# GpSimd keeps its part of the modulation sum in an accumulator of its own

## The chip, the core and the metric

The kernel runs on one core of a Trainium2 chip. The core's engines each run their own instructions in a fixed order: TensorE (PE, with its weight loads as PEld), VectorE (DVE), ScalarE (ACT), GpSimd (POOL) and SyncE (SP), which issues most of the transfers. The metric is the device time of one execution in microseconds (us); lower is better.

## The reference, cut to what matters

Two layers of a backbone over 512 latent tokens and 256 context tokens of width 1024. Ahead of each layer a modulation vector is computed from the conditioning, once for the latents and once for the context; it scales and shifts the normalised input and gates the layer's output. In the second layer only the latents go on to the output, so the gate part of its modulation is needed for them alone.

```
mod = silu(c) @ mod_w + mod_b          # 1024 -> 3 x 1024: shift, scale, gate; also for c_ctx
h   = rmsnorm(x) * (1 + scale) + shift
z   = h @ w_in                          # one projection: attention, pool, GLA, gates, merge
y_m = softmax_attention(...) * silu(z_mla_gate)     # 8 heads
y_p = multiscale_pool(...)   * silu(z_pool_gate)
y_g = gla_scan(...)          * silu(z_gla_gate)     # both directions
merged = sum over branches b of sigmoid(z_merge_b) * (y_b @ w_branch_b)
x   = x + gate * rmsnorm(merged @ w_out)
```

## The kernel before

Everything is kept in fp32 precision: an operand is split into a high and a low half (wh, wl), and a product is three matmuls. Each layer runs through stages: input projection, gated linear attention (GLA) with the pooling mixer, the softmax attention, the merge of the three branches, the output projection. Within a stage the parts of several kinds of work are interleaved: beside the attention of layer l, PE computes the blocks of the merge gates (zA_m), whose weights come as 512 KB blocks raw_m through SP, are split by ACT (wh_m) and DVE (wl_m), and leave PE by way of ACT (st_m) and a transfer (sm).

The modulation of a layer has twelve chunks of 256 columns, j = 0 to 11; j = 8 to 11 are the gate. Layer 0's first eight are done by PE at the start. The other sixteen are done "beside PE" (`chunk_beside_pe`, L210): layer 0's j = 8 to 11 and layer 1's j = 0 to 7 for two streams (latents and context), layer 1's j = 8 to 11 for one. A chunk is eight tiles of 128 rows of mod_w, brought as two loads of 512 KB (raw_mod). Each tile is multiplied by a column of silu(c) and added into the accumulator macc. DVE does multiply and add in one instruction; POOL takes the odd tiles of the last stream and does a multiply in place (raw_mod, L230) and an add (macc). Both add into the same accumulator, so each waits for the other at every step. At the end PE sums the accumulator over its 128 partitions by a matmul with a column of ones (modt), two per stream. `columns` (L167) adds the bias; for the gate chunks it also writes the result to a buffer in DRAM, grow, by one transfer for each stream on POOL's queue (L179), element by element. The output stage reads it back as pg (L264).

The steps of these chunks are drawn by hand from a generator, `next(todo_mod)`. Drawing a step starts a chunk (its loads and its sums) and finishes the one before it (modt, columns, grow). In layer 0 there is a step after all but a few of the 24 gate blocks (the condition at L911) and one after the last, sixteen in all; in layer 1 a step after each of the four pairs of blocks of the p branch (L998) and one after the branches (L1001). From the emitted program a scheduler makes the engines' orders, with priorities (`urgent`) and a pool's buffers as limits: a tile of a pool with n buffers must wait until the n-th last one of its name is free.

Three pools matter here. `stream` has three buffers under the name raw, through which go raw_m, raw_mod, the branches' weights (raw_wbp, raw_wbg, raw_wbm) and the branches' inputs as they are read back (yrp, yrg, yrm). `small` lasts for the whole program and holds macc. `att{l}` is opened with the attention of layer l (L740) and holds, among much else, ys (two buffers), a half of a head's output on its way from PSUM to ypair.

Of the kernel before, what the change touches and what calls it, by code (L numbers as in the profile page):

```python
# [11 lines left out]
F32 = mybir.dt.float32  # L12
# [6 lines left out]
P = 128  # L19
D = 1024  # L20
KD = 8
# [27 lines left out]
def hybrid_kernel(ctx, tc, io, out):  # L49
# [23 lines left out]
    def stt(out, a, s, b, op0=ALU.mult, op1=ALU.mult):  # L73
        return V.scalar_tensor_tensor(out=out, in0=a, scalar=s, in1=b, op0=op0, op1=op1)  # L74
# [29 lines left out]
    def load_raw(src, nk, width, name, pool=stream):  # L104
        raw = pool.tile([P, nk, width], F32, tag="raw", name=f"raw_{name}", bufs=3 if pool is stream else None)
        nc.sync.dma_start(out=raw, in_=src)
        return raw
# [46 lines left out]
    def modulation(l, pool=None):  # L154


        cols = const.tile([P, 24, 2], F32, tag=f"mcols{l}", name=f"mcols{l}")
        grow = dram.tile([2, D], F32, name=f"grow{l}")
        mods[l] = (cols, grow)
        modb = small.tile([P, 24], F32, tag="modb", name=f"modb{l}", bufs=1)  # L160
        nc.gpsimd.dma_start(out=modb, in_=io["mod_b"][l])
        pre = small.tile([P, KD], F32, tag="pre", name=f"pre{l}", bufs=1)
        nc.gpsimd.dma_start(out=pre, in_=io["pre_norm"][l])
        post = small.tile([P, KD], F32, tag="post", name=f"post{l}", bufs=1)
        nc.gpsimd.dma_start(out=post, in_=io["post_norm"][l])

        def columns(j, pt, streams=2):  # L167

            at = slice(2 * j, 2 * j + 2)
            dst = cols[:, at, 0:streams]  # L170

            def spread(v, c0):
                return v[:, 2 * j - c0:2 * j - c0 + 2].unsqueeze(2).to_broadcast([P, 2, streams])

            tt(dst, pt[:, :, 0:streams], spread(modb, 0), ALU.add)
            if j >= 8:
                tt(dst, dst, spread(post, 16))
                for st in range(streams):
                    nc.gpsimd.dma_start(out=grow[st].rearrange("(b p) -> p b", p=P)[:, 2 * j - 16:2 * j - 14], in_=dst[:, :, st])  # L179
            elif j >= 4:  # L180

                stt(dst, dst, 1.0, spread(pre, 8), ALU.add, ALU.mult)

        def chunk_on_pe(j):
            parts = j in (5, 6, 3, 7)
            ps = pst.tile([4 if parts else 2, 256], F32, tag="t", name=f"modps{l}_{j}")
            for half in range(2):
                raw = pool.tile([P, 4, 256], F32, tag="raw", name=f"raw_mod{l}_{j}_{half}", bufs=10)
                nc.sync.dma_start(out=raw, in_=io["mod_w"][l, j][:, 4 * half:4 * half + 4, :])
                if parts:  # L190
                    wh = pool.tile([P, 4, 256], F32R, tag="xin", name=f"mwh{l}_{j}_{half}", bufs=6)
                    wl = pool.tile([P, 4, 256], F32R, tag="xin", name=f"mwl{l}_{j}_{half}", bufs=6)
                    act(wh, raw)
                    tt(wl, raw, wh.bitcast(F32), ALU.subtract)
                for k in range(4):
                    kk = 4 * half + k
                    if parts:
                        mm(ps, chl[:, kk, :], wh[:, k, :], kk == 0, False)
                        mm(ps[0:2], chl[:, kk, 0:2], wl[:, k, :], False, kk == KD - 1)
                    else:  # L200
                        mm(ps, csil[:, kk, :], raw[:, k, :], kk == 0, kk == KD - 1)
            n = 4 if parts else 2
            row = pool.tile([n, 256], F32, tag="modrow", name=f"modrow{l}_{j}")
            act(row, ps)
            pt = psz.tile([P, 2, 2], F32, tag="z", name=f"modt{l}_{j}")
            for i in range(2):
                mm(pt[:, i], row[:, i * P:(i + 1) * P], sel[0:n], True, True)
            columns(j, pt)

        def chunk_beside_pe(j):  # L210

            streams = 2 if j < 8 or l < DEPTH - 1 else 1
            acc = small.tile([P, 2, 256], F32, tag="macc", name=f"macc{l}_{j}", bufs=1)
            for half in range(2):
                raw = load_raw(io["mod_w"][l, j][:, 4 * half:4 * half + 4, :], 4, 256, f"mod{l}_{j}_{half}")
                for k in range(4):
                    kk = 4 * half + k
                    for st in range(streams):
                        c = csil[:, kk, st:st + 1]
                        w, a = raw[:, k], acc[:, st]  # L220
                        eng = (G if streams == 1 and kk%2 else V) if st==0 else (G if kk%2 else V)
                        if kk == 0:
                            (eng if eng is G else V).tensor_scalar(out=a, in0=w, scalar1=c, scalar2=None, op0=ALU.mult)
                        elif eng is V:
                            stt(a, w, c, a, ALU.mult, ALU.add)
                        else:
                            if eng is S:
                                act(w, w, scale=c)
                            else:
                                G.tensor_scalar(out=w, in0=w, scalar1=c, scalar2=None, op0=ALU.mult)  # L230
                            tt(a, a, w, ALU.add, G)
            yield
            pt = psz.tile([P, 2, 2], F32, tag="z", name=f"modt{l}_{j}")
            for i in range(2):
                for st in range(streams):
                    mm(pt[:, i, st:st + 1], acc[:, st, i * P:(i + 1) * P], ones, True, True)
            columns(j, pt, streams)


        pend = []  # L240
        for j in (0, 4, 1, 5, 2, 6, 3, 7, 8, 9, 10, 11):
            if pool is not None and j < 8:
                chunk_on_pe(j)
            else:
                pend.append(chunk_beside_pe(j))
                next(pend[-1])
                if len(pend) > 1:
                    next(pend.pop(0), None)
            if j == 11 or (pool is None and j == 7):
                yield  # L250
                for chunk in pend:
                    next(chunk, None)
                pend = []
            yield

    mods = {}

    def gate_rows(l, pool, streams):

# [89 lines left out]
    def layer(l, hT, close_hT, side, todo_mod):  # L349
# [387 lines left out]


        g2 = ExitStack()
        ap = g2.enter_context(opened(f"att{l}", 2, side))  # L740
        pss = g2.enter_context(opened(f"pss{l}", 1, None, MemoryType.PSUM))
        psu = g2.enter_context(opened(f"psu{l}", 2, None, MemoryType.PSUM))
        qn = ap.tile([P, 2], F32, tag="qn", name=f"qn{l}", bufs=1)
# [114 lines left out]
        def weighted_sum(head, q0, nk):  # L858
            pth, ptl = pt_h.pop((head, q0))
            j = head % 2  # L860
            vv = vvs[head // 4]
            av = pst.tile([P, 256], F32, tag="t", name=f"av{l}_{head}_{q0}")
            for kt in range(nk):
                st_ = vv[:, kt, head % 4].rearrange("p s d -> p (s d)")
                mm(av, st_, pth[:, kt, :], kt == 0, False)
                mm(av, st_, ptl[:, kt, :], False, kt == nk - 1)
            if (head, q0) == (head, groups[0][0]) and j == 0:
                yps[head // 2] = ap.tile([P, T], F32, tag="ypair", name=f"ypair{l}_{head // 2}", bufs=1)
            ypair = yps[head // 2]
            rows = slice(64 * j, 64 * j + 64)  # L870
            oth = slice(64 - 64 * j, 128 - 64 * j)
            ys = ap.tile([P, 256], F32, tag="ys", name=f"ys{l}_{head}_{q0}")
            act(ys[rows], av[oth])
            tt(ypair[rows, q0 * P:q0 * P + 256], av[rows], ys[rows], ALU.add)
            if j == 1 and q0 == groups[-1][0]:
                pair = head // 2
                sg = ap.tile([P, T], F32, tag="qf", name=f"sgm{l}_{pair}", bufs=1)
                nc.gpsimd.dma_start(out=sg[:, lo:T], in_=sg_d["m"][pair][:, lo:T])
                tt(ypair[:, lo:T], ypair[:, lo:T], sg[:, lo:T])
                if full or pair < 3:  # L880
                    nc.gpsimd.dma_start(out=y_d["m"][pair][:, lo:T], in_=ypair[:, lo:T])
# [26 lines left out]
        for nm in ("m1", "m2", "m0"):  # L908
            for i in range(8):
                gate_block(nm, i, sm_d[nm], tanh_out if nm in early_gates else stage_out)  # L910
                if full and n_mod >= 6 and n_mod % 6 != 3:  # L911
                    next(todo_mod, None)
                n_mod += 1

# [331 lines left out]
```

## Time and profile before

| | |
|---|---|
| runs shown | 1511.17, 1519.75 and 1519.8 us; median 1519.75 us |
| the profiled execution | 1523.7 us, of it 1521.9 us from the first to the last instruction |
| mean granted TensorE clock | 0.982 of full speed |

The stages and how busy PE is in them, by the windows of the trace:

| us | stage | PE busy | PE clock |
|---|---|---|---|
| 0 to 60 | start, modulation on PE | 50.12 | 1.00 |
| 60 to 425 | layer 0: projection, GLA, pooling mixer | 360.92 | 0.99 to 1.00 |
| 425 to 720 | layer 0: attention, gate blocks, p branch begins | 273.20 of 295 | 0.97 |
| 720 to 870 | layer 0: branches, output | 146.61 of 150 | 1.00 |
| 870 to 1340 | layer 1: up to its attention | 458.95 of 470 | 0.99 |
| 1340 to 1410 | layer 1: p and g branches beside the attention's end | 59.17 of 70 | 0.90 |
| 1410 to 1522 | layer 1: branches, output | 100.08 of 112 | 0.98 |

In the prediction, a row of a group reads: line, engine, operation, tile written <- tiles read, shape, count | busy us, mean ns of one | idle us of the engine just before them, and the releaser that ended most of it. In a timeline row the first number is the start, the second the length, and the square bracket is the idle time before it. A transfer's number is the time from issue to landing.

### The profile page before, as it was taken

Reading aid. Unit: us, or ns where it says so; the run is one execution under the profiler, and the core shown is the slowest. Engines: PE = TensorE matmul, PEld = TensorE weight load, DVE = VectorE, ACT = ScalarE, POOL = GpSimd, SP = SyncE. Lnnn points to the kernel's source line nnn. Section 1 sums busy time; section 2 is a strip of 40 time slices with the busy share of each in tenths; the row PEclk is TensorE's granted clock in tenths of the full one; section 3 lists DMA queues with packets and bytes.
Section 4 is the critical chain, followed back from the end, with each engine's and each line's share of the span. In section 5 each row is a group of like instructions: output and inputs, shape, how many; then the busy total and the mean of one; then the engine's idle time right before and its main releaser. Section 6 shows DMA issues by size and latency. Waiting matters only on the chain. (4 is left out here: it accounts for less than half of the span.)

```text
span 1521.9 us, 23904 instructions
## 1 busy us (share of the span) xinstructions
PE 1449.1 (95%) x8940; PEld 1282.7 (84%) x8940; DVE 1069.9 (70%) x1980; ACT 718.5 (47%) x1340; POOL 525.4 (35%) x695
## 2 busy tenths in 40 slices
PE   7999999999997999998999989999999999997988
PEld 3799899998886889887879978988988888886878
DVE  3645999757575788876675374689976676686783
ACT  6554453443343445656443346554253555454532
POOL 3431433454243344552111074424553000063450
PEclk9999999999998999999999999999999999998999
DMA  9333333255544632446555233434256423158631
GB/s 366 105 118 118 101 101 115 89 165 191 180 77 99 140 121 89 137 139 183 172 196 201 79 116 117 155 117 126 90 177 215 153 95 95 51 156 152 222 127 68
DMA packets 64195, 209.75 MB, mean 138 GB/s; under 512 B 12464, under 2 KB 15696, under 8 KB 64080
## 3 DMA queue, kind: packets, MB, share of 16 engines
q1 hardware_dynamic: 38688, 116.74, 25.3%
q0 software_dynamic: 24528, 88.34, 18.0%
q10 hardware_dynamic: 864, 3.15, 0.5%
q8 instruction: 70, 1.15, 0.3%
q14 instruction: 45, 0.37, 0.1%
HBM read 161.65 MB, written 46.54 MB: 137 GB/s over the span
## 5 line engine op out<-in xcount | busy, mean ns | idle before, releaser
L89 PE MATMUL zA_m<-hh,wh_m 128*128 128x512 f32 (+1 forms) x576 | 206.3, 358 | 1.1 <-ACT wh_m L68 1.1
L89 PE MATMUL zA_m<-hh,wl_m 128*128 128x512 f32 (+1 forms) x576 | 205.9, 358 | 0.6 <-DVE wl_m L71 0.6
L89 PE MATMUL zA_m<-hl,wh_m 128*128 128x512 f32 (+1 forms) x576 | 206.3, 358 | 0.0
L89 PEld LDWEIGHTS zA_m<-hh,wh_m 128*128 128x128 f32 x576 | 109.7, 190 | 16.0 <-ACT wh_m L68 1.5
L89 PEld LDWEIGHTS zA_m<-hh,wl_m 128*128 128x128 f32 x576 | 109.5, 190 | 15.4 <-DVE wl_m L71 1.1
L89 PEld LDWEIGHTS zA_m<-hl,wh_m 128*128 128x128 f32 x576 | 109.6, 190 | 14.3
L68 ACT ACTIVATE wh_m<-raw_m 128x1024 fp32r<-128x1024 f32 x48 | 50.9, 1060 | 93.4 <-PE zA_m L89 40.7
L68 ACT ACTIVATE pe<-sc,mx 128x768 f32<-128x768 f32 (+1 forms) x80 | 65.2, 815 | 61.3 <-DVE mx L830 60.7
L71 DVE TENSOR_TENSOR wl_m<-raw_m,wh_m 128x1024 fp32r<-128x1024 f32 x48 | 58.9, 1226 | 47.1 <-ACT wh_m L68 46.6
L230 POOL TENSOR_SCALAR raw_mod<-raw_mod,csil 128x256 f32<-128x256 f32 x64 | 70.5, 1106 | 61.5 <-DVE macc L74 39.4
L830 DVE TENSOR_REDUCE mx<-sc 128x1 f32<-128x768 f32 (+1 forms) x80 | 67.6, 845 | 34.1 <-PE sc L89 33.5
L74 DVE SCALAR_TENSOR_TENSOR macc<-raw_mod,csil,macc 128x256 f32<-128x256 f32 x132 | 71.6, 552 | 10.9 <-POOL macc L71 9.2
L68 ACT ACTIVATE pth<-pt 128x256 fp32r<-128x256 f32 (+1 forms) x144 | 62.0, 472 | 31.9 <-PE pt L852 31.4
L71 DVE TENSOR_TENSOR ptl<-pt,pth 128x256 fp32r<-128x256 f32 (+1 forms) x144 | 72.5, 533 | 6.0 <-ACT pth L68 4.8
L89 PEld LDWEIGHTS lv<-pqk 128*128 128x128 f32 x560 | 70.9, 191 | 4.6 <-issue 1.8
L89 PE MATMUL lv<-pqk 128*128 128x128 f32 x560 | 73.4, 275 | 1.2 <-DVE pqk L71 1.1
L346 POOL DMA_DIRECT2D sm<-st_m x32 | 17.6, 550 | 161.9 <-ACT st_m L68 144.5
L89 PE MATMUL sc<-kth,qth 96*128 96x256 f32 (+1 forms) x144 | 50.4, 350 | 24.0 <-ACT pe L68 24.0
L71 POOL TENSOR_TENSOR macc<-macc,raw_mod 128x256 f32<-128x256 f32 x64 | 55.5, 868 | 35.5 <-DVE macc L74 29.8
L89 PE MATMUL br_p<-yp,wh_wbp 128*128 128x512 f32 (+1 forms) x192 | 56.6, 379 | 6.7 <-ACT yp L68 5.8
L852 PE MATMUL pt<-ident,pe 128*128 128x128 f32 x416 | 61.3, 273 | 0.3 <-DVE pe L839 0.2
L89 PE MATMUL zB_gv<-wh_gv,hh 128*128 128x256 f32 x192 | 55.3, 290 | 5.1 <-ACT st_gv L68 2.9
(402 smaller groups left out, 4746.2 us busy)
## 6 DMA issues: line engine op xcount, KB each, us to landing
raw_mod<-in_mod_w SPq DMA_DIRECT2D x48, 512.0 KB, 5.2
raw_m<-in_w_in SPq DMA_DIRECT2D x48, 512.0 KB, 3.7
sm<-st_m POOLq DMA_DIRECT2D x24, 384.0 KB, 3.0
raw_wo<-in_w_out SPq DMA_DIRECT2D x16, 512.0 KB, 3.9
sm<-st_m POOLq DMA_DIRECT2D x24, 256.0 KB, 2.5
raw_gv<-in_w_gv SPq DMA_DIRECT2D x8, 512.0 KB, 3.8
raw_gg<-in_w_in SPq DMA_DIRECT2D x8, 512.0 KB, 4.0
raw_px<-in_w_in SPq DMA_DIRECT2D x8, 512.0 KB, 4.0
```

The costliest lines, as they stand in the source:

```text
L68: return S.activation(out=out, in_=in_, func=func, **kw)
L71: return (eng or V).tensor_tensor(out=out, in0=a, in1=b, op=op)
L74: return V.scalar_tensor_tensor(out=out, in0=a, scalar=s, in1=b, op0=op0, op1=op1)
L89: PE.matmul(out=out, lhsT=lhsT, rhs=rhs, start=start, stop=stop)
L230: G.tensor_scalar(out=w, in0=w, scalar1=c, scalar2=None, op0=ALU.mult)
L346: nc.gpsimd.dma_start(out=dst[:, lo:T], in_=st[:, lo:T])
L830: V.tensor_reduce(out=mx, in_=ps[:, 0:nkey], axis=AX.X, op=ALU.max, negate=True)
L852: PE.transpose(out=pt[:, kk, :], in_=pe[:, (k0 + kk) * P:(k0 + kk + 1) * P], identity=ident)
```

## The change

The accumulator gets a third row, acc[:, 2]. Where the last stream's tile is odd, POOL multiplies the first one (kk = 1) into that row and adds the later ones to it; DVE's part stays in acc[:, st]. PE puts the two together with a second matmul into the same result. macc moves from the pool `small` to the attention's pool, reached through `beside[0]`; with three rows it is 3 KB a partition, and ys there gets one buffer for two. The condition on the steps in layer 0 is another: it leaves out the first four blocks and every third, so that fourteen steps are drawn there, not sixteen. The chunks j = 8 and 9 of layer 1 thereby begin in layer 1's p branch, and j = 11 is finished by the last step, after the branches.

```diff
-            acc = small.tile([P, 2, 256], F32, tag="macc", name=f"macc{l}_{j}", bufs=1)
...
+            acc = beside[0].tile([P, 3, 256], F32, tag="macc", name=f"macc{l}_{j}", bufs=1)
+            for kk in range(KD):
+                if kk % 4 == 0:
+                    raw = load_raw(io["mod_w"][l, j][:, kk:kk + 4, :], 4, 256, f"mod{l}_{j}_{kk // 4}")
+                w = raw[:, kk % 4]
+                for st in range(streams):
+                    c = csil[:, kk, st:st + 1]
+                    if st == streams - 1 and kk % 2:
+                        a = acc[:, 2]
+                        G.tensor_scalar(out=a if kk == 1 else w, in0=w, scalar1=c, scalar2=None, op0=ALU.mult)
+                        if kk > 1:
                             tt(a, a, w, ALU.add, G)
+                    elif kk == 0:
+                        V.tensor_scalar(out=acc[:, st], in0=w, scalar1=c, scalar2=None, op0=ALU.mult)
+                    else:
+                        stt(acc[:, st], w, c, acc[:, st], ALU.mult, ALU.add)
             yield
             pt = psz.tile([P, 2, 2], F32, tag="z", name=f"modt{l}_{j}")
             for i in range(2):
+                at = slice(i * P, (i + 1) * P)
                 for st in range(streams):
-                    mm(pt[:, i, st:st + 1], acc[:, st, i * P:(i + 1) * P], ones, True, True)
+                    both = st == streams - 1
+                    mm(pt[:, i, st:st + 1], acc[:, st, at], ones, True, not both)
+                    if both:
+                        mm(pt[:, i, st:st + 1], acc[:, 2, at], ones, False, True)
             columns(j, pt, streams)
...
+    beside = [None]
...
-        ap = g2.enter_context(opened(f"att{l}", 2, side))
+        ap = beside[0] = g2.enter_context(opened(f"att{l}", 2, side))
...
-            ys = ap.tile([P, 256], F32, tag="ys", name=f"ys{l}_{head}_{q0}")
+            ys = ap.tile([P, 256], F32, tag="ys", name=f"ys{l}_{head}_{q0}", bufs=1)
...
-                if full and n_mod >= 6 and n_mod % 6 != 3:
+                if full and n_mod >= 4 and n_mod % 3 != 2:
                     next(todo_mod, None)
```

What this does to the engines' orders is seen at three places. The first is ACT in layer 0's attention, just after the second gate chunk (j = 9) has been finished and its two grow transfers issued. Before:

```order
L68 ACTIVATE ys_0_2_4103<-av_0_2_4089 64x256
L68 ACTIVATE wh_m_0_6521<-raw_m_0_6519 128x1024
L68 ACTIVATE pe_0_4_1_3970,sm_0_4_1_3971<-sc_0_4_1_3961,mx_0_4_1_3968 128x768
L68 ACTIVATE qth_1_4047<-qf_1_4026 96x768
L68 ACTIVATE st_m_0_6515<-zA_m_0_256_6465 128x512
```

And with the change:

```order
L68 ACTIVATE pe_0_4_0_3955,sm_0_4_0_3956<-sc_0_4_0_3946,mx_0_4_0_3953 128x768
L68 ACTIVATE wh_m_0_6462<-raw_m_0_6460 128x1024
L68 ACTIVATE st_m_0_6456<-zA_m_0_256_6406 128x512
L68 ACTIVATE pe_0_4_1_3970,sm_0_4_1_3971<-sc_0_4_1_3961,mx_0_4_1_3968 128x768
L68 ACTIVATE qf_1_4026<-qps_1_256_4027 64x512
```

In both, the split of a freshly loaded weight block (wh_m) stands ahead of the exponentials (pe) of the same piece of the attention; the chunk now ends somewhat earlier in the attention.

The second is SP at the end of layer 0, where the last mod loads, the first weights of the p branch (raw_wbp) and its inputs (yrp) follow one another. Before:

```order
L106 DMA raw_m_0_7602<-in_w_in 128x1024
L106 DMA raw_mod_8_0_7663<-in_mod_w 128x1024
L106 DMA raw_mod_8_1_7671<-in_mod_w 128x1024
L106 DMA raw_mod_9_0_7680<-in_mod_w 128x1024
L106 DMA raw_mod_9_1_7688<-in_mod_w 128x1024
L106 DMA raw_wbp_0_7714<-in_w_branch_p 128x1024
L934 DMA yrp_0_7720<-yp_552 128x768
```

With the change:

```order
L106 DMA raw_mod_7_0_7574<-in_mod_w 128x1024
L106 DMA raw_mod_7_1_7585<-in_mod_w 128x1024
L106 DMA raw_m_0_7605<-in_w_in 128x1024
L106 DMA raw_wbp_0_7686<-in_w_branch_p 128x1024
L938 DMA yrp_0_7692<-yp_552 128x768
```

The four loads of layer 1's chunks 8 and 9 have left this place.

The third is SP in layer 1's p branch, from its last yrp on. Before:

```order
L934 DMA yrp_3_14619<-yp_9671 128x512
L106 DMA raw_mod_10_0_14657<-in_mod_w 128x1024
L106 DMA raw_mod_10_1_14665<-in_mod_w 128x1024
L106 DMA raw_wbp_1_14679<-in_w_branch_p 128x1024
L106 DMA raw_wq_7_13468<-in_w_uq 128x256
L106 DMA raw_mod_11_0_14718<-in_mod_w 128x1024
L106 DMA raw_mod_11_1_14726<-in_mod_w 128x1024
L106 DMA raw_wbp_2_14740<-in_w_branch_p 128x1024
L106 DMA raw_wbp_3_14784<-in_w_branch_p 128x1024
L106 DMA raw_wbg_0_14822<-in_w_branch_g 128x1024
```

With the change:

```order
L106 DMA raw_mod_8_1_14636<-in_mod_w 128x1024
L106 DMA raw_wbp_1_14644<-in_w_branch_p 128x1024
L106 DMA raw_wq_7_13440<-in_w_uq 128x256
L106 DMA raw_mod_9_0_14683<-in_mod_w 128x1024
L106 DMA raw_mod_9_1_14690<-in_mod_w 128x1024
L106 DMA raw_wbp_2_14706<-in_w_branch_p 128x1024
L106 DMA raw_mod_10_0_14745<-in_mod_w 128x1024
L106 DMA raw_mod_10_1_14752<-in_mod_w 128x1024
L106 DMA raw_wbp_3_14768<-in_w_branch_p 128x1024
L106 DMA raw_mod_11_0_14807<-in_mod_w 128x1024
L106 DMA raw_mod_11_1_14814<-in_mod_w 128x1024
L106 DMA raw_wbg_0_14830<-in_w_branch_g 128x1024
```

Two mod loads now stand between any two weight blocks of the p branch. On POOL the grow of layer 1's last chunk, which stood within the branches, now stands behind the four ml subtractions ahead of the output projection, and pg directly behind it.

More of the change, by code (lines that the diff above doesn't have):

```diff
@@ L212, in chunk_beside_pe @@
             streams = 2 if j < 8 or l < DEPTH - 1 else 1
-            acc = small.tile([P, 2, 256], F32, tag="macc", name=f"macc{l}_{j}", bufs=1)
[L214 to L230, printed above, removed]
+            acc = beside[0].tile([P, 3, 256], F32, tag="macc", name=f"macc{l}_{j}", bufs=1)
[9 more added lines that the diff above has]
+                        if kk > 1:
                             tt(a, a, w, ALU.add, G)
+                    elif kk == 0:
+                        V.tensor_scalar(out=acc[:, st], in0=w, scalar1=c, scalar2=None, op0=ALU.mult)
+                    else:
+                        stt(acc[:, st], w, c, acc[:, st], ALU.mult, ALU.add)
             yield
```

## The prediction

> **What bounds the kernel now.** I read the page from the top: engine shares first, then the groups with the idle time ahead of them.
>
> ```profile
> span 1521.9 us, 23904 instructions
> PE 1449.1 (95%) x8940; PEld 1282.7 (84%) x8940; DVE 1069.9 (70%) x1980; ACT 718.5 (47%) x1340; POOL 525.4 (35%) x695
> L230 POOL TENSOR_SCALAR raw_mod<-raw_mod,csil 128x256 f32<-128x256 f32 x64 | 70.5, 1106 | 61.5 <-DVE macc L74 39.4
> L74 DVE SCALAR_TENSOR_TENSOR macc<-raw_mod,csil,macc 128x256 f32<-128x256 f32 x132 | 71.6, 552 | 10.9 <-POOL macc L71 9.2
> L89 PE MATMUL sc<-kth,qth 96*128 96x256 f32 (+1 forms) x144 | 50.4, 350 | 24.0 <-ACT pe L68 24.0
> L71 POOL TENSOR_TENSOR macc<-macc,raw_mod 128x256 f32<-128x256 f32 x64 | 55.5, 868 | 35.5 <-DVE macc L74 29.8
> L89 PE MATMUL br_p<-yp,wh_wbp 128*128 128x512 f32 (+1 forms) x192 | 56.6, 379 | 6.7 <-ACT yp L68 5.8
> ```
>
> PE is busy 95% of the span, so only what adds PE work or opens and closes its 73 us of gaps can move the time. GpSimd's waits in the shared accumulator look large (39.4 + 29.8 us), but PE does not wait for them: the groups with idle time on PE are sc (24.0 us, behind ScalarE's pe) and br_p (5.8 us, behind ScalarE's yp). So I asked where these two sit, through the waits, the timeline and the transfers of the windows around them.
>
> ```profile
> PE sc L89 <- ACT pe L68: 10.8, 1, 10.8
> 463.90 1.06 ACT L68 ACTIVATE wh_m<-raw_m 128x1024 fp32r<-128x1024 f32 x1 [14.43 <-DMA raw_m<-in_w_in]
> 464.98 0.90 ACT L68 ACTIVATE pe<-sc,mx 128x768 f32<-128x768 f32 x1
> DMA to landing us min/median/max: 3.1/3.7/16.6
> L179 POOL DMA_DIRECT2D grow<-mcols x12: 716/741/776, 428.8 to 1392.3; - x12
> DMA to landing us min/median/max: 4.0/9.2/16.6
> ```
>
> The first row is PE's wait at 466 us, the longest of sc. ScalarE runs in order: it stood 14.43 us at wh_m for a weight load, with the pe that PE needed queued behind. That load, issued at 447 us, is the longest of its kind: 16.6 us, where raw_m takes 3.7 us at the median (fourth row, the tile view of raw_m). The last two rows are the tile view of grow: twelve writes of one KB or less, one element of four bytes at a time, with a median landing of 9.2 us (the three pg loads are counted in it) and one of 16.6. A pair of them was in the air at 446 us. The other gaps have the same neighbour:
>
> ```profile
> yrp<-yp SPq DMA_DIRECT2D x4, 384.0 KB, 6.4
> grow<-mcols POOLq DMA_DIRECT2D x1, 1.0 KB, 9.0
> 699.95 0.50 PE L89 MATMUL sc<-kth,qth 96*128 96x512 f32 x1 [1.15 <-ACT pe L68]
> 707.91 1.52 PE L89 MATMUL br_p<-yp,wh_wbp 128*128 128x512 f32 x3 [5.60 <-ACT yp L68]
> 1369.58 11.55 DMA raw_wbp<-in_w_branch_p
> 1383.14 0.80 PE L89 MATMUL sc<-kth,qth 96*128 96x512 f32 x1 [5.38 <-ACT pe L68]
> 1392.05 9.82 DMA raw_wbg<-in_w_branch_g
> 1403.88 0.50 PE L89 MATMUL sc<-kth,qth 96*128 96x512 f32 x1 [2.53 <-ACT pe L68]
> 466.03:470.30 4.27, 4.27 (x18) 4.08 (x19) 3.79 (x9) 1.82 (x5) 2.03 (x2) 0.50 0.37 123
> 705.90:712.70 6.80, 4.79 (x14) 4.07 (x15) 5.58 (x12) 5.37 (x12) 0.72 (x1) 0.50 0.84 277
> 1381.70:1391.90 10.20, 8.36 (x23) 6.82 (x24) 9.38 (x14) 7.86 (x15) 5.40 (x5) 0.50 0.56 151
> 1405.60:1409.00 3.40, 3.40 (x9) 2.67 (x8) 3.40 (x6) 2.00 (x3) 2.24 (x4) 0.50 0.89 257
> ```
>
> Rows 1 and 2 are transfers issued between 690 and 712 us, at the end of layer 0. Rows 5 and 7 are pieces of the chain of waits in layer 1's branches. The last four are the windows table (us, PE busy, PEld, DVE, ACT, POOL, granted clock, DMA share, GB/s): after each long gap the granted clock is 0.50, and half of PE's busy time there is loss. The price of a place is its gap plus this half: at 446 us 10.8 + 2.1 = 12.9 us; at 696 us 1.15 + 5.60 + 2.4 = 9.2 us; in layer 1 5.38 + 2.53 + 4.2 + 1.7 = 13.8 us, for three grows, 4.6 each. So my reading is: grow writes hold up the loads issued behind them, and a load that ScalarE meets in its order stops PE. The change is worth what it does to these places.
>
> **The change part by part.**
>
> *Sixteen POOL adds fewer.* The first odd tile's product now is the accumulator: 64 adds become 48, 16 x 0.868 = 13.9 us of POOL, which is 35% busy. The mutual waits go (9.2 us on DVE; POOL's are not on PE's path). PE gains at most what sc waits outside the places above: 24.0 - 10.8 - 1.15 - 5.38 - 2.53 = 4.1 us, and DVE's other work stays. Bounds 0 and -4.1; I take -2, the middle, since no row ties these waits to macc.
>
> *The sum of the two accumulators on PE.* Two more matmuls a chunk, 32 in all, each seen as two rows:
>
> ```profile
> L89 PE MATMUL modt<-ones,macc 128*128 128x1 f32 x112 | 14.1, 237 | 0.0
> ```
>
> Before there are 56 matmuls in 112 rows, so 64 rows come. By busy time a row costs 14.1/112 = 0.126 us: +8.1 us. Bounds: 0 if they fell into gaps, 64 x 0.237 = 15.2 if none overlapped. PE is 95% busy and they stand in its order: +8.1.
>
> *macc in the attention's pool.* The chunk j=8 of layer 0, which before began in the pooling mixer, cannot begin until that pool opens.
>
> ```profile
> L223 DVE TENSOR_SCALAR macc<-raw_mod,csil x28: 325/346/428, 368.8 to 1364.5; 128x256 f32<-128x256 f32 x28
> 368.00:425.00 57.00, 57.00 (x334) 50.31 (x334) 35.38 (x66) 22.62 (x37) 19.97 (x27) 1.00 0.51 172
> 368.00:640.00 272.00, 257.18 (x1591) 228.88 (x1591) 206.61 (x423) 124.44 (x262) 112.56 (x131) 0.97 0.46 123
> ```
>
> PE had no gap from 368 to 425 us, so nothing is gained there. DVE's part of this chunk, 14 x 0.552 + 2 x 0.346 = 8.4 us, moves into a stretch where DVE is already busy 206.61 of 272. Between 0 and +8.4: +1, nearer to nothing, since a tenth or so of DVE's delay has reached PE (the 9.2 us above against PE's small waits).
>
> *ys in one buffer.* The next ys waits for the add that reads the last one.
>
> ```profile
> L71 DVE TENSOR_TENSOR ypair<-av,ys x40: 397/422/429, 454.0 to 1453.4; 64x256 f32<-64x256 f32 x40
> ```
>
> Behind a waiting ys on ScalarE stand pe and pth. The wait is at most one add, 0.42 us: 0 to 40 x 0.42 = 17 us. I take 0, because the 40 come over a thousand us, some 25 us apart at the mean.
>
> *The pairs of layer 0's attention (j = 8 to 11).* Four pairs remain. In the order, the weight loads stand behind the second pair as before, so I keep one hit and shorten it: 16.6 was the longest landing; at 9.2 ScalarE is released 7.4 us sooner, which leaves 10.8 - 7.4 + 2.1 = 5.5 us, and 2 more for small hits of the other three. 7.5 against 12.9: -5. Bounds: -12.9 (none hit) and +12.9 (another one hit in full).
>
> *The end of layer 0.* Two chunks (layer 1's j = 8 and 9) leave it: four 512 KB loads ahead of raw_wbp and yrp in SP's queue, and the one grow behind which yrp landed late. ScalarE's yp and then br_p come sooner. 0 to -9.2; -9.2, because yrp has nothing else to wait for.
>
> *Layer 1's branches.* SP now brings eight mod loads between the p branch's four weight loads, not four, through the same ring of three; three grows (j = 8, 9, 10) stay, the last one goes to the end.
>
> ```profile
> 1361.21 1.24 POOL macc L71
> 1362.46 3.97 DMA raw_wbp<-in_w_branch_p
> raw_mod<-in_mod_w SPq DMA_DIRECT2D x48, 512.0 KB, 5.2
> 1340.00:1410.00 70.00, 59.17 (x307) 49.64 (x306) 52.21 (x95) 34.06 (x66) 32.71 (x38) 0.90 0.70 162
> ```
>
> The first two rows, from the chain: a weight load issued only when POOL's last macc gave a ring slot back. Four more loads can cost 0 to 4 x 5.2 = 20.8 us; PE is idle 10.8 of these 70 us, so much of that is exposed already. I take one load, +5. The grows at their old price: 0.
>
> *The last grow.* It stands on POOL's queue behind the last ml, with pg behind it.
>
> ```profile
> 1472.37 1.60 POOL L71 TENSOR_TENSOR ml<-acc,mh 128x512 fp32r<-128x512 f32 x1 [1.89 <-ACT mh L68]
> DMA to landing us min/median/max: 4.0/4.5/4.7
> L71 DVE TENSOR_TENSOR part<-part,pg x4: 684/691/695, 1484.9 to 1494.0; 128x512 f32<-128x512 f32 x4
> 1491.45 1.23 DVE L71 TENSOR_TENSOR wl_wo<-raw_wo,wh_wo 128x1024 fp32r<-128x1024 f32 x1 [0.67 <-ACT wh_wo L68]
> ```
>
> 1474.0 + 9.2 + 4.5 (pg, second row) = 1487.7, 2.8 us after the first part add. Three adds of 0.69 then end at 1489.8, ahead of wl_wo at 1491.45, on which PE depends: 0. At 16.6 it is 1495.1 and costs up to 5.7.
>
> Sum: -2 + 8.1 + 1 + 0 - 5 - 9.2 + 5 + 0 = -2.1 us on the profiled execution, whose run took 1523.7 us. The median of the runs shown is 1519.75, so 1517.6 us.
>
> **The rivals.**
>
> *B, slower: layer 1's ring jams.* If the four loads are exposed whole, layer 1 costs 20.8 instead of 5, 15.8 more: 1533.4. If the last grow before the g branch also holds yrg as the one at 1369 held raw_wbp (5.38 + 4.2 = 9.6), 1543.0. Middle 1538. For it: the slot wait in the chain, and PE idle there already. Against: each chunk gives its slot back sooner. It decides once PE waits over 15 us more in these branches.
>
> *C, faster: no grow meets a load that matters.* The pairs cost 0 (-12.9, not -5) and layer 1's half (-6.9, not +5): 1517.6 - 7.9 - 11.9 = 1497.8. For it: before there were grows at eight places (four pairs, four single ones), and PE's long gaps stand at four. Against: the loads still follow the grows closely.
>
> *D: layer 0's end gains nothing,* because yrp is held by another wait: 1526.8. Against it stands the 9.0 us grow beside a yrp of 6.4.
>
> *E: the two accumulators block each other.* Uncoupled, POOL's multiplies and DVE's accumulation run at the same time more often. In the trace DVE's instruction spans 552 ns at the mean:
>
> ```profile
> L74 DVE SCALAR_TENSOR_TENSOR macc<-raw_mod,csil,macc x132: 457/479/1550, 370.4 to 1383.5; 128x256 f32<-128x256 f32 x132
> ```
>
> so all slowing now is at most 132 x (552 - 457) = 12.5 us. If each one met half of a POOL add (0.43 us), it would be 57 us, 45 more on DVE; at the tenth that has reached PE, +4.5 instead of -2: 1524.1. The Trainium skill's page "SBUF — State Buffer", section "Who interferes with whom", speaks against the change in this way: a VectorE instruction with two SBUF inputs contends with a GpSimd instruction that reads SBUF, and the loser of the port stands still for the whole instruction. By that rule the sum would be E's; the median of 479 ns beside the 1550 ns longest shows that it happens, but not to half of the instructions.
>
> **How the numbers follow.** The likeliest, 0.43, is 1517.6, with 1508 to 1528 its own range. B 0.21, C 0.24, D 0.06, E 0.06. The range 1495 to 1541 takes in C's value and B's middle, and leaves out about a third of each, 0.15. A measurement of this kernel tells about 1% (15.2 us) from no change: faster is below 1504.6, slower above 1535. Faster: 0.20 of C and 0.05 of the likeliest's tail, 0.25. Slower: 0.16 of B and 0.03 of D, E and the rest, 0.19. Same: 0.56.
>
> **What would show it.** modt has 176 rows of about 22 us in all; POOL's macc adds number 48 and nothing waits DVE to POOL on macc; br_p waits no 5.6 us at layer 0's end and yrp lands in some 3 us; a load behind a grow still takes 9 us or more. Layer 1's 70 us become 75, with raw_wbp issued when a mod slot is freed. The forecast is wrong if PE's long waits stand somewhere else, above all if a pair of grows meets other loads than before, or if pg is late at the end.

## The result, and the profile after

| | before | after |
|---|---|---|
| median of the runs | 1519.78 us (4 runs) | 1542.56 us (1540.85 to 1549.89, 4 runs) |
| span of the profiled execution | 1521.9 us | 1541.9 us |
| granted clock | 0.982 | 0.979 |

The ratio is 1.0167 with a 95% interval of 1.0135 to 1.0199: slower by some 22.8 us. The forecast was 1517.6 us; the result lies just above the range.

The head of the page after, and of its groups those that answer to the ones shown of before:

```profile
span 1541.9 us, 24019 instructions
PE 1461.4 (95%) x9004; PEld 1291.9 (84%) x9004; DVE 1070.3 (69%) x1980; ACT 718.4 (47%) x1340; POOL 504.2 (33%) x679
L223 POOL TENSOR_SCALAR raw_mod<-raw_mod,csil 128x256 f32<-128x256 f32 x48 | 54.0, 1127 | 70.7 <-DVE macc L74 56.5
L74 DVE SCALAR_TENSOR_TENSOR macc<-raw_mod,csil,macc 128x256 f32<-128x256 f32 x132 | 68.2, 540 | 0.9
L89 PE MATMUL br_p<-yp,wh_wbp 128*128 128x512 f32 (+1 forms) x192 | 54.6, 370 | 6.1 <-ACT wh_wbp L68 4.6
L89 PE MATMUL modt<-ones,macc 128*128 128x1 f32 x176 | 21.6, 236 | 0.5 <-POOL macc L71 0.4
```

The change does what it says: DVE's idle time ahead of its accumulation falls from 10.9 to 0.9 us, and POOL is 21 us less busy. POOL's multiply still waits for DVE, because it overwrites a tile that DVE, for the other stream, must have read. PE's own waits (the waits view; us in total, times, longest) have moved:

```profile
PE sc L89 <- ACT pe L68: 7.8, 6, 4.3
PE pt L856 <- ACT pe L68: 7.6, 1, 7.6
PE zB_wo L89 <- DVE mcols L71: 7.2, 1, 7.2
PE zA_m L89 <- ACT wh_m L68: 4.9, 2, 4.4
PE br_p L89 <- ACT wh_wbp L68: 4.6, 1, 4.6
```

The one wait of 10.8 us is gone, and so is br_p's wait of 5.8 us for yp; five others of 4 to 8 us have come.

To see where the time came from I cut each execution at work that every version does: at the first sc of layer 0, the first transpose for layer 1, the last zA_m of layer 1 and the last br_m. "Stalls" is PE's idle time, plus half of PE's busy time where the granted clock is 0.5; "work" is the rest.

| piece (us) | before: length = stalls + work | after |
|---|---|---|
| start to layer 0's attention | 426.5 = 17.1 + 409.5 | 425.9 = 16.6 + 409.3 |
| layer 0: attention, branches, output | 447.3 = 31.5 + 415.9 | 449.8 = 27.8 + 422.0 |
| layer 1 up to its last gate block | 460.0 = 15.4 + 444.6 | 459.1 = 13.2 + 445.9 |
| layer 1: p branch to the last br_m | 128.7 = 17.3 + 111.5 | 141.4 = 26.9 + 114.5 |
| to the end | 59.3 = 11.3 + 48.0 | 65.7 = 18.4 + 47.3 |

Of 20 us in the spans, 12.7 lie in layer 1's branches and 6.4 behind them. Layer 0, where the prediction had most of the gain, is 2.5 us longer: 6.1 us more work, and only 3.7 us fewer stalls. The pieces are of one profiled execution each. The changed kernel and the kernel of the second experiment below (PSUM) have the same orders up to layer 1's branches, and yet their first two pieces differ by 2.0 and 3.3 us; a difference of that size between two kernels says little.

### The profile page after: what moved, and what is told of

It reads as the page before. It is cut to its first block, busy times and chain, and to the rows that moved or that the text cites. A ratio compares the mean times of both kernels' runs of the same rounds, so it can differ in the third digit from the quotient of the medians.

```text
span 1541.9 us, 24019 instructions
## 1 busy us (share of the span) xinstructions
PE 1461.4 (95%) x9004; PEld 1291.9 (84%) x9004; DVE 1070.3 (69%) x1980; ACT 718.4 (47%) x1340; POOL 504.2 (33%) x679
## 4 chain that ended last, share of the span: by engine, by line
PE 63%; DVE 16%; DMA 9%; issue 5%; POOL 3%; ACT 3%; SPq 0%; DVEq 0%; POOLq 0%; ACTq 0%
PE zA_m L89 15%; PE zB_gv L89 4%; PE zB_wo L89 4%; PE zA_mg L89 4%; DMA raw_m<-in_w_in 4%; PE wo L89 3%; PE sc L89 3%; PE zA_pg L89 2%; PE zA_gk L89 2%; PE br_m L89 2%; PE lv L89 2%; PE zA_px L89 2%; PE br_p L89 2%; DVE pqk L71 2%; PE zB_qkv L89 2%
## 5 line engine op out<-in xcount | busy, mean ns | idle before, releaser
L89 PEld LDWEIGHTS zA_m<-hl,wh_m 128*128 128x128 f32 x576 | 109.3, 190 | 14.4
L223 POOL TENSOR_SCALAR raw_mod<-raw_mod,csil 128x256 f32<-128x256 f32 x48 | 54.0, 1127 | 70.7 <-DVE macc L74 56.5
L74 DVE SCALAR_TENSOR_TENSOR macc<-raw_mod,csil,macc 128x256 f32<-128x256 f32 x132 | 68.2, 540 | 0.9
L856 PEld LDWEIGHTS pt<-ident,pe 128*128 128x128 f32 x416 | 50.9, 145 | 14.2 <-ACT pe L68 7.8
L89 PE MATMUL br_g<-yg,wh_wbg 128*128 128x512 f32 (+1 forms) x192 | 55.1, 367 | 4.4 <-ACT yg L68 3.2
```

The costliest lines, as they stand in the source:

```text
L89: PE.matmul(out=out, lhsT=lhsT, rhs=rhs, start=start, stop=stop)
L223: G.tensor_scalar(out=a if kk == 1 else w, in0=w, scalar1=c, scalar2=None, op0=ALU.mult)
L856: PE.transpose(out=pt[:, kk, :], in_=pe[:, (k0 + kk) * P:(k0 + kk + 1) * P], identity=ident)
```

## The experiments

**First question: is it the steps or the accumulator?** The theory was that the moved steps (theory S) make the loss. One kernel has the accumulator with the steps of before, one the steps with the accumulator of before.

```diff
 (own accumulator, old steps)
-            acc = beside[0].tile([P, 3, 256], F32, tag="macc", name=f"macc{l}_{j}", bufs=1)
+            acc = small.tile([P, 2, 256], F32, tag="macc", name=f"macc{l}_{j}", bufs=1)
+            if streams == 2:
+                own = beside[0].tile([P, 256], F32, tag="macg", name=f"macg{l}_{j}", bufs=1)
+            else:
+                own = acc[:, 1]
...
-                if full and n_mod >= 4 and n_mod % 3 != 2:
+                if full and n_mod >= 6 and n_mod % 6 != 3:
 (the kernel before, new steps)
-                if full and n_mod >= 6 and n_mod % 6 != 3:
+                if full and n_mod >= 4 and n_mod % 3 != 2:
```

> GpSimd's own accumulator, the second matmul and the single ys buffer stay; the steps are drawn as before (16 in layer 0). Because layer 1's chunks 8 and 9 then begin in layer 0, macc stands in the small pool as before and only the two-stream chunks' third row in the attention's pool. Theory S (the moved steps cost the 22.8 us, in layer 1's branches +12.6 and behind them +6.4): 1516 to 1529 us, layer 1's stretch from the p branch to the last br_m back at some 126 us. Rival A (the accumulators, the doubled matmul and ys cost it): 1535 us or more.

> The kernel before with the new condition on the steps alone (14 in layer 0), shared accumulator. S: 1532 to 1545 us, with layer 1's last grow behind ml at the end. A: 1514 to 1525 us.

| | time (us) | ratio to before | layer 0: length, stalls | layer 1's branches | end |
|---|---|---|---|---|---|
| own accumulator, old steps | 1529.12 | 1.0076 (1.0045 to 1.0106) | 445.0, 22.1 | 138.9, 25.6 | 59.6 |
| new steps alone | 1535.20 | 1.0122 (1.0085 to 1.0159) | 433.5, 16.1 | 157.1, 44.3 | 61.8 |

Each half alone is slower, so neither theory holds as it stood: the new steps alone came out as S had it (1532 to 1545 us), but the first run ended at the edge of what S allowed, and layer 1's branches did not come back. The new steps alone do in layer 0 what the prediction said and more (15.4 us fewer stalls), and lose 28 us in layer 1. The own accumulator with the old steps also lengthens layer 1's branches by 10 us, where only the two chunks of before stand. Its transfers between 1350 and 1395 us (the transfers view; the last number is the median to landing):

```profile
raw_wbg<-in_w_branch_g SPq DMA_DIRECT2D x4, 512.0 KB, 7.3
yrg<-yg SPq DMA_DIRECT2D x4, 256.0 KB, 9.8
raw_wbm<-in_w_branch_m SPq DMA_DIRECT2D x1, 512.0 KB, 10.0
grow<-mcols POOLq DMA_DIRECT2D x3, 1.0 KB, 9.1
```

Three grows, and the loads beside them late: three of the four yrg, which before took 2.7 us, took over 9.

**Is PE held by the last chunk's PSUM tile?** zB_wo waits 7.2 us for mcols, since the tile of the last modt must be read before its slot is free.

```diff
-            pt = psz.tile([P, 2, 2], F32, tag="z", name=f"modt{l}_{j}")
+            late = l == DEPTH - 1 and j == 11
+            pt = (pst if late else psz).tile([P, 2, 2], F32, tag="t" if late else "z", name=f"modt{l}_{j}")
```

> The changed kernel; only the PSUM tile of the very last chunk's column sums (layer 1, j = 11) comes from another pool, so that the output projection's first tile need not wait for mcols, which stands behind DVE's merge additions. If that slot is what holds PE 7.2 us at the end: 1534 to 1538 us and no wait of zB_wo on mcols. If the merge's last additions are late anyway: within 2 us of 1542.6, the wait then on ml or mgt_late.

1543.43 us (ratio to before 1.0168), the end 65.9 us: no gain. The wait on mcols is gone, and another has its place: zB_wo now waits 5.3 us for DVE's gated. The timeline of this run, POOL and DVE (start, length, line, operation):

```profile
1467.98 0.56 POOL L269 DMA_DIRECT2D pg<-grow  x1 [4.95 <-DMA grow<-mcols]
1468.54 2.11 POOL L1064 DMA_DIRECT2D xres<-x_d  x4
1470.65 1.30 POOL L71 TENSOR_TENSOR acc<-acc,gated 128x512 f32<-128x512 f32 x1
1471.89 2.57 POOL L71 TENSOR_TENSOR acc<-acc,mgt_late 128x512 f32<-128x512 f32 x2
1474.39 1.31 POOL L71 TENSOR_TENSOR ml<-acc,mh 128x512 fp32r<-128x512 f32 x1
1475.63 1.28 POOL L71 TENSOR_TENSOR acc<-acc,gated 128x512 f32<-128x512 f32 x1
1476.85 1.27 POOL L71 TENSOR_TENSOR ml<-acc,mh 128x512 fp32r<-128x512 f32 x1
1470.01 9.21 DVE L71 TENSOR_TENSOR wl_wo<-raw_wo,wh_wo 128x1024 fp32r<-128x1024 f32 x1
```

POOL stands 4.95 us at pg until the late grow has landed, then does what had queued behind it without a break, and through about that time DVE's wl_wo takes 9.21 us, where instructions of its size take 1.2 when POOL is idle; then gated, for which PE waits, comes late. The Trainium skill's page "SBUF — State Buffer", section "Who interferes with whom", has it that a VectorE instruction with two SBUF inputs and a GpSimd one that reads SBUF exclude each other, and that the loser stands still; this row agrees, and suggests that a run of GpSimd instructions, here six, can keep VectorE out through all of them. It need not: most instructions of this size that overlap with POOL in this run take 1.2 us too.

**What is the memory of the attention's pool worth?** In the changed kernel mh, whose memory opens when the attention's closes, begins as the last modt ends. This timeline is of the changed kernel:

```profile
1476.44 0.95 PE L89 MATMUL modt<-ones,macc 128*128 128x1 f32 x8
1484.54 0.55 PE L89 MATMUL zB_wo<-wh_wo,mh 128*128 128x256 f32 x1 [7.16 <-DVE mcols L71]
1477.37 3.21 ACT L68 ACTIVATE mh<-acc 128x512 fp32r<-128x512 f32 x6
1479.02 4.78 DVE L71 TENSOR_TENSOR acc<-acc,mgt_late 128x512 f32<-128x512 f32 x1
1479.53 3.71 POOL L71 TENSOR_TENSOR ml<-acc,mh 128x512 fp32r<-128x512 f32 x3
```

Six mh came at once, then three ml on POOL without a break, and DVE's addition beside them took 4.78 us for 0.69. Behind that addition in DVE's order stands mcols, for which zB_wo waits. The last grow and pg come later here, at 1488.9 and 1497.0 us, and delay nobody: pg has landed at 1501.9 us, and the first part, at 1504.6, waited for ScalarE. The next kernel is the changed one with macc in the small pool again, as in the first diff but with the new steps.

> The changed kernel, its steps too, but macc stands in the small pool again and only the two-stream chunks' third row in the attention's pool, so that layer 1's last chunks don't hold the attention's memory, on which mh waits until the last modt. Theory M (that hold makes the end long: mh began only when modt had ended): 1533 to 1538 us, from the last br_m to the end 59 to 61 us, not 65.7. Rival (the late grow and pg make the end long): 1540 us or more, the end still 64 us or more.

1530.77 us, ratio to before 1.0062 (1.0042 to 1.0082): 11.8 us less than the changed kernel, more than expected. The end takes 61.7 us for 65.7, just above the 59 to 61 that theory M gave, and mh begins ahead of the last modt:

```profile
1462.23 1.75 ACT L68 ACTIVATE mh<-acc 128x512 fp32r<-128x512 f32 x3
1468.09 0.95 PE L89 MATMUL modt<-ones,macc 128*128 128x1 f32 x8
```

So the hold on mh explains 4.0 us. Most of the rest lies ahead of layer 1: layer 0 takes 444.5 us for 449.8 and the start 2.6 us less, together 7.9 us (6.7 us less than in the PSUM run). What in the place of macc costs there was not looked into. The end is still 2.4 us over before, as it is with the new steps alone (61.8 us).

**What do the element-wise writes cost?** Two small matmuls turn the gate columns into rows, and grow is written as runs of 512 bytes. The same edit was made in the changed kernel, in the kernel before, in the one with own accumulator and old steps, and in the one with macc in the small pool and the new steps.

```diff
-                for st in range(streams):
-                    nc.gpsimd.dma_start(out=grow[st].rearrange("(b p) -> p b", p=P)[:, 2 * j - 16:2 * j - 14], in_=dst[:, :, st])
+                gt = psz.tile([2, streams, P], F32, tag="z", name=f"growt{l}_{j}")
+                for st in range(streams):
+                    mm(gt[:, st], dst[:, :, st], ident, True, True)
+                gr = acc[0:2, 0, 0:streams * P].rearrange("b (s p) -> b s p", p=P)
+                V.tensor_copy(out=gr, in_=gt)
+                for st in range(streams):
+                    nc.gpsimd.dma_start(out=grow[st].rearrange("(b p) -> b p", p=P)[2 * j - 16:2 * j - 14], in_=gr[:, st])
```

> The changed kernel with the gate columns turned by two small matmuls into rows, so that grow is written as two runs of 512 bytes per stream, not 256 elements of 4 bytes. If the element-wise writes hold up the loads behind them: grow lands in 2 to 4 us, raw_wbp, raw_wbg, yrg and raw_m issued beside it in 3 to 6 us, and the time falls to 1510 to 1530 us. If the ring of three buffers and the eight loads themselves make the loss: 1538 us or more.

> The kernel before, with grow written as two runs of 512 bytes per stream (turned into rows by two small matmuls) in place of four-byte elements. Theory G (the element-wise writes hold up the loads behind them, worth the 35.9 us that the prediction read at three places, of which other waits take some back): 1495 to 1508 us, raw_m, yrp and raw_wbp beside a grow landing in 3 to 6 us. Rival (the gaps have another cause): 1515 us or more.

> GpSimd's own accumulator with the old steps, as in the run with the old steps, and grow by rows. G: layer 1's branches, which were 10 us longer there than in the kernel before, come back, and the time is 1505 to 1517 us. Rival (the accumulator itself delays these branches): 1524 us or more.

> Own accumulator, macc in the small pool, the new steps, grow by rows. If the new steps only trade layer 0's end against layer 1's branches (1.6 us between the two runs with element-wise grow): 1505 to 1513 us, as with the old steps. If the eight loads in layer 1's ring cost by themselves: 1516 us or more, with layer 1's branches at 135 us or more.

| with grow by rows | time (us) | ratio to before | layer 0: length, stalls | layer 1's branches | end |
|---|---|---|---|---|---|
| the changed kernel | 1537.20 | 1.0135 (1.0101 to 1.0169) | 442.1, 15.8 | 139.8, 22.7 | 67.8 |
| the kernel before | 1513.56 | 0.9940 (0.9921 to 0.9959) | 438.9, 16.0 | 125.7, 11.5 | 61.1 |
| own accumulator, old steps | 1507.81 | 0.9906 (0.9879 to 0.9933) | 437.4, 9.5 | 123.9, 10.2 | 60.7 |
| macc small, new steps | 1524.39 | 1.0040 (1.0019 to 1.0062) | 435.0, 10.6 | 140.3, 23.1 | 62.4 |

The tile view of grow, of before with the rows, reads

```profile
DMA to landing us min/median/max: 1.5/2.6/6.0
```

for 4.0/9.2/16.6. (Both count three pg; the twelve writes alone have a median of 2.3 us for 9.5.) That the writes hold up the loads is seen in all the traces together. I take the 512 KB weight loads of mod, gate blocks and branches and the loads of the branches' inputs that SP issued 1 to 6 us after a grow and whose landing the trace has. In the eight kernels with element-wise grow there are 62, and every one took 7.5 to 11.6 us; in the five with rows there are 24, and they took 2.6 to 5.4 us. In the kernel before the stalls fall by 15.5 us in layer 0 and 5.8 in layer 1, 21 of the 35.9 that the prediction had put down to grow; work grows by some 10 us by the same table of pieces (the turning matmuls are 4.5 us of it; the rest is not explained), so the time falls by 6 to 7 only, and the expectation of 1495 to 1508 was missed, as was the 1510 to 1530 for the changed kernel. With the own accumulator and the old steps it falls by 21 us, as expected: its 10 us in layer 1 were collisions of grows with loads. The third row is faster than both kernels, and 5.8 us faster than the second row: with the grows out of the way, and at the old steps, the own accumulator is a gain, though it brings the doubled sum.

The changed kernel gained only 5 us, and the last row tells why: with the new steps layer 1's branches stay at 140 us though no grow takes over 4.5 us, as the rival of that run had it. The last two rows differ in the steps alone. The tile view in this stretch shows the issues of raw_wbg and the matmuls of the g branch (count: ns min/median/max, first and last start); first the old steps, whose stretch begins at 1324.4 us:

```profile
L106 SPq DMA_DIRECT2D raw_wbg<-in_w_branch_g x4: 328/330/333, 1368.0 to 1389.0; - x4
L89 PE MATMUL br_g<-yg,wh_wbg x64: 387/389/477, 1392.9 to 1424.1; 128*128 128x512 f32 x64
```

and the new ones, from 1321.1 us on:

```profile
L106 SPq DMA_DIRECT2D raw_wbg<-in_w_branch_g x4: 327/330/333, 1389.9 to 1409.5; - x4
L89 PE MATMUL br_g<-yg,wh_wbg x64: 388/389/628, 1401.2 to 1434.8; 128*128 128x512 f32 x64
```

SP's waits of its weight loads for macc with the new steps, from 1325 to 1410 us (us in total, times, longest):

```profile
SPq L106 <- DVE macc L74: 21.6, 3, 12.0
SPq L106 <- POOL macc L71: 10.4, 3, 7.8
```

and with the old steps, from 1325 to 1400 us:

```profile
SPq L106 <- DVE macc L74: 14.6, 2, 11.2
```

From the stretch's start the g branch's first weights are asked for after 43.6 us with the old steps and after 68.8 with the new, and the branch begins after 68.5 and 80.1 us. SP waits 32 us in all for macc to give a buffer of the ring back, and 14.6 with the old steps. PE meanwhile does the attention's last heads: the last sc starts 58 us before the stretch's end with the new steps and 32 us before it with the old, so the g and m branches run with less beside them. That this is what makes the stretch longer is my reading and not shown: in the kernel before with the rows, whose stretch is short with 125.7 us, the last sc starts 46 us before its end, and in the changed kernel, where it takes 141.4 us, 33 us before. Nor was a ring of four buffers tried, so the ring is not separated from the work that DVE and POOL do for the two chunks more.

**ys and the doubled matmuls.** One kernel is the kernel before with a single buffer for ys; another the changed kernel in which POOL adds the two accumulators, so that PE sums one.

```diff
 (the kernel before)
-            ys = ap.tile([P, 256], F32, tag="ys", name=f"ys{l}_{head}_{q0}")
+            ys = ap.tile([P, 256], F32, tag="ys", name=f"ys{l}_{head}_{q0}", bufs=1)
 (the changed kernel)
+            tt(acc[:, streams - 1], acc[:, streams - 1], acc[:, 2], ALU.add, G)
             yield
...
-                    mm(pt[:, i, st:st + 1], acc[:, st, at], ones, True, not both)
-                    if both:
-                        mm(pt[:, i, st:st + 1], acc[:, 2, at], ones, False, True)
+                    mm(pt[:, i, st:st + 1], acc[:, st, at], ones, True, True)
```

> The kernel before with one buffer for ys. If the single buffer costs nothing, as the prediction had it: 1517 to 1523 us. If ScalarE loses an add at each of the 40: 1525 to 1537 us.

1521.04 us, ratio 0.9993 (0.9969 to 1.0017): ys costs nothing.

> The changed kernel, but POOL adds its accumulator to DVE's at the end of a chunk (16 adds more), and PE sums only the one: 32 matmuls fewer. If the doubled matmuls cost what the prediction took, 8 us: 1533 to 1538 us, and the PE work at full clock in layer 0's attention and branches some 5 us less. If they were hidden: 1540 to 1545 us.

1533.27 us, ratio to before 1.0083 (1.0059 to 1.0107): 9.3 us less than the changed kernel. Layer 0's work falls from 422.0 to 417.1 us for 44 rows of modt, 0.11 us a row, and PE's work in all pieces by 6.6 us; modt's busy time falls from 21.6 to 14.4 us. So nearly all of the doubled sum is on PE's path. The rest of the 9.3 us is stalls, 3.9 of them in layer 0, whose order has changed too.

Last, the best version with this POOL sum (own for acc[:, 2]) and the rows turned by PE's transpose.

```diff
-                    mm(gt[:, st], dst[:, :, st], ident, True, True)
+                    PE.transpose(out=gt[:, st], in_=dst[:, :, st], identity=ident)
```

> The best version so far (own accumulator, old steps, grow by rows; 1507.8 us) with POOL's final add in place of the second matmul, and the rows turned by PE's transpose. If the doubled matmuls cost PE 7 us there too: 1499 to 1504 us. If POOL's extra add delays modt instead: 1506 us or more.

1513.90 us, ratio to before 0.9957 (0.9934 to 0.9981), a miss: 6 us slower than without. Layer 0's work fell by 8.5 us, but its stalls went from 9.5 to 22.0, more than the matmuls saved. PE does not wait at modt in this run, so the recorded alternative, that POOL's extra add delays modt, isn't seen; the longest waits of that piece are two of br_p, 3.2 us for yp and 1.6 us for acc, at 712 and 718 us, with the granted clock at 0.5 from 707 to 724 us. Whether the added step, the transposes or the order brings them wasn't tried.

## Why the prediction was wrong

*The direction* followed from two gains in layer 0 (5 and 9.2 us) against 5 us in layer 1. The two gains were not had together, and layer 1 and the end cost more. By the pieces, layer 0 was to gain some 9 us (-5 - 9.2 and 44 of the 64 rows of modt, +5.5) and lost 2.5; layer 1's branches, with their +5, lost 12.7, and the end, with 0, lost 6.4.

*Right.* The doubled sum: +8.1 us forecast; modt's busy time rose from 14.1 to 21.6 us, and the work of the pieces behind the start grows by 6.1 + 1.3 + 3.0 - 0.7 = 9.7 us, in which other work that moved between the pieces is counted. ys: 0. That grow holds up the loads behind it: grow by rows took 21 us of stalls from the kernel before. That layer 0's end is freed: br_p's 5.60 us wait fell to 1.46, and with the new steps alone layer 0 lost 15.4 us of stalls. With the half clock the place costs 3.2 us in the changed kernel, so -6.0 and not -9.2; and behind it br_m now waits 3.3 us for mgt_g, at 769 us.

*The mutual waits of POOL and DVE, -2: not settled.* They went, as forecast, but no run has that alone. With grow by rows and the old steps the own accumulator took 5.8 us off although it doubles the sum, so its worth can be more than the 4.1 us that I had as the bound.

*The pairs of layer 0's attention, -5: failed.* I let one pair hit and the others graze. Two hit, by the timeline of ACT after:

```profile
438.63 1.06 ACT L68 ACTIVATE wh_m<-raw_m 128x1024 fp32r<-128x1024 f32 x1 [4.68 <-DMA raw_m<-in_w_in]
516.64 1.06 ACT L68 ACTIVATE wh_m<-raw_m 128x1024 fp32r<-128x1024 f32 x1 [7.17 <-DMA raw_m<-in_w_in]
```

Neither was behind the second pair, as I had read from the order: the two loads were issued 7.0 and 7.9 us after the first and the fourth pair and took 8.2 and 9.6 us. PE was idle 4.4 and 4.3 us, and at half clock it was busy 4.26 and 3.40 us just after. By the same price as before that is 8.7 + 3.8 = 12.5 us for 12.9: these give back what the one place had saved.

*macc in the attention's pool, +1: failed.* I priced the late start of one chunk, and with a slip: DVE's part of it is 10 accumulations, not 14 (132 = 12 x 10 + 4 x 3), which makes 6.2 us, not 8.4. With macc in the small pool the changed kernel is 11.8 us faster. What I had not seen is the other end of the pool's life: memory that opens when the attention's closes waits for the last modt, which the moved step had put behind all branches. That is 4.0 us, at the end. The 7 to 8 us ahead of layer 1 lie where I had looked, and their mechanism stays open.

*Layer 1's branches, +5: mis-sized.* The term named the right place, the ring of three, and took one load of 5.2 us. The stretch grew by 12.7 us; with grow's delays out of the way the new steps cost 16.4 us (140.3 against 123.9), not far from the 20.8 us which I had as the upper bound. In the changed kernel itself the long gaps there are still grows': ScalarE stood 6.9 us at wh_wbp and 7.2 at wh_wbg for loads issued 4.1 and 2.3 us after a grow, PE was idle 4.6 and 7.6 us, and with half of 11.1 us at half clock that is 17.8 us, where I had kept the 13.8 of before. The changed kernel is not worse by the sum of the new steps' loss and the grows': with the old steps and the own accumulator the grows alone made this stretch 138.9 us. The two don't add; that a load can be late for one reason at a time would explain it, but is not shown. The own accumulator itself is no loss here: with the new steps and element-wise grow the stretch is 157.1 us with the shared accumulator and 141.4 with the own one.

*The last grow, 0: failed.* I followed pg to its reader, part, and found slack there, and in the changed kernel that slack was there. The cost is ahead of the grow: the last chunk's mcols, which zB_wo needs out of its PSUM slot, stood in DVE's order behind an addition that took 4.78 us beside POOL's three ml, and PE waited 7.2 us. With another slot (the PSUM run) POOL's queue behind pg took its place. Of the 6.4 us, 4.0 go with the place of macc; the 2.4 that are left come with the new steps alone too (61.8 us).

*Rival B* was the nearest, 1538 us with a chance of 0.21, but its condition, over 15 us more waiting in the branches, was not met: the stalls there grew by 9.6. Much of the rest came with the place of macc. Rival E's exclusion of DVE by POOL is real, but at the end of the kernel, not in the accumulation, where the mean went from 552 to 540 ns.

## What to carry to other kernels

When a buffer is moved to another pool, look at both ends of that pool's life: what its last reader now holds back. When work is moved to a place where loads share a small ring, ask when the next stage's first load is issued, not how many loads there are. And follow a late instruction through its own engine's order: here what stood ahead of mcols on DVE, and beside it on POOL, mattered, not the reader of what came of it.

## What the runs showed of the hardware

Writes of four-byte elements cost far more in what stands behind them than in themselves: 1 KB took 9.5 us at the median, and all 62 loads of the kinds above that SP issued 1 to 6 us after such a write took 7.5 us or more; the same bytes in runs of 512 took 2.3 us, and none of 24 such loads behind them took over 5.5. A load issued at nearly the same moment can still get ahead: in the changed kernel a raw_mod issued 0.1 us after a grow took 4.0 us. The Trainium skill's page "DMA: Bandwidth & Descriptors", section "Queues, rings and completion order", says that the semaphore write of a transfer lands only after every earlier write of that DMA engine, across its queues; the late loads agree with it, but no run here separates late data from a late signal. And POOL can shut DVE out through several instructions in a row: 9.21 us for an instruction of 1.2 beside six of them, 4.78 for one of 0.69 beside three.
